# Reading the moving operand of the wide matrix products backwards, and writing their output backwards

## The chip, the cores and the metric

The kernel runs on one core of one Trainium2 chip. The metric is the device time of one execution in microseconds (us), as the median of several executions. The engines have short names in the profile: PE is TensorE (its matmuls), PEld its weight loads, DVE is VectorE, ACT is ScalarE, POOL is GpSimd, SP is SyncE, which here issues the DMAs.

## The reference: what is computed

Two layers of a streaming-encoder trunk over a sequence of 256 rows of 2048 features, all in float32. Each layer projects the input, runs three groups of heads (differential attention, banded chunk attention and an mLSTM), projects their outputs back, and adds a SwiGLU block, with a layer norm after each:

```
for li in range(DEPTH):                                   # DEPTH = 2
    proj = x @ w_in[li]
    ...
    mix = jnp.concatenate([ya, yb, yc], axis=-1) @ w_out[li]
    x = layer_norm(DEEPNORM_ALPHA * x + mix, ln1_g[li], ln1_b[li])
    ffn = (jax.nn.silu(x @ w_gate[li]) * (x @ w_up[li])) @ w_down[li]
    x = layer_norm(DEEPNORM_ALPHA * x + ffn, ln2_g[li], ln2_b[li])
```

## The kernel before

Five large weight matrices per layer (w_in, w_out, w_gate, w_up, w_down) are streamed once from memory. The output columns of each product are handled in groups of up to 1024 columns, and a group is two blocks: 512 and 512 columns nearly everywhere, 512 and 264 in the second group of w_in of each layer. The 256 rows of the sequence are two tiles t of 128. `run_groups` walks over the groups one after the other. Within a group a step k is one slice of 128 rows of the weights. For step k, `convert` brings the slice into a form of two parts: ScalarE writes the rounded upper part `whi` (line 225), VectorE the remainder `wlo` (line 226), both of type fp32r. The activations stand ready in the same two parts, transposed: `xth` and `xtl` (from x or from the mixed heads), or `gth` and `gtl` (from the SwiGLU gate).

The wide products are all issued by one line, 273. For each step and tile there are three part products (upper by upper, upper by remainder, remainder by upper), each on both blocks, so six instructions, which all add into the blocks' PSUM banks `mm`:

```
for i, (lt, wt) in enumerate(((xh, hi), (xh, lo), (xl, hi))):
    for b in bs:
        o, w = g["blocks"][b]
        nc.tensor.matmul(banks[t, b][:, 0:w], lt, wt[:, o:o + w],
```

The 128x128 activation block `lt` is the stationary operand, loaded by a weight load of its own ahead of each product. The weight block `wt`, 128 partitions by up to 512 columns, is the moving operand: its columns stream past the stationary one, and each column of it makes one column of output. When the last step of a bank is done, ScalarE or VectorE empties it. In most of a group the two blocks alternate, so that consecutive products go to different banks; in the last steps of a group (`so` of them) the order is by block, and consecutive products add into one bank.

Between the wide products the kernel's task list (`Tasks`) puts the small ones on TensorE: transposes (lines 296, 415, 649, 742) and the products of the heads (lines 520, 543, 550 to 552, 626, 672 to 674, 716, 750), which are plain float32 and go to banks named `aux`. Line 633 adds, on VectorE, a bias that is stored reversed: it reads `brev` with a step of -1; line 725 does the same operation in the other attention with a bias read forwards. Line 172 issues nine products on zeros at the very start.

What sets the order is the list of groups and steps written out in `run_groups`; every engine works through its own instruction queue in that order and waits only on data.

Of the kernel before, what the change touches and what calls it, by code (L numbers as in the profile page):

```python
# [135 lines left out]
class Trunk:  # L136
# [96 lines left out]
    def run_groups(self, groups):  # L233

        nc = self.nc
        self.steps, self.pairs, self.raws, self.whl = [], [], {}, {}
        for g in groups:
            g["base"] = len(self.steps)
            for k in range(g["nk"]):
                self.steps.append((g, k))  # L240
                if k % 2 == 0:
                    self.pairs.append(g["src"](k))
        for p in range(RAW_BUFS):
            self.load_pair(p)
            for c in {1: (1,), 2: (2, 3)}.get(p, ()):
                for t in range(NT):
                    self.load_x(nc.sync, t, c)
        done = 0
        for g in groups:
            nk, nb, si, so = g["nk"], len(g["blocks"]), g.get("skew_in", 1), g.get("skew_out", 1)  # L250
            allb = tuple(range(nb))
            order = [(k, t, allb) for t in range(NT) for k in range(si)]
            order += [(k, t, allb) for k in range(si, nk - so) for t in range(NT)]
            order += [(k, t, (b,)) for t in range(NT) for b in allb for k in range(nk - so, nk)]
            banks = {}
            g["start"]()
            for (k, t, bs) in order:
                j = g["base"] + k
                if (k, t, bs[-1]) == (nk - 1, NT - 1, nb - 1) and "mid" in g:
                    g["mid"]()  # L260
                xh, xl = g["lhs"](k, t)
                ahead = AHEAD if k >= nk - so or k < si else FAR_AHEAD
                while done < min(j + ahead + 1, len(self.steps)):
                    self.convert(done)
                    done += 1
                hi, lo = self.whl[j]
                for b in bs:
                    if (t, b) not in banks:
                        banks[t, b] = self.psum.tile([P, 512], F32, name="mm", tag="mm", bufs=MM_BUFS)
                for i, (lt, wt) in enumerate(((xh, hi), (xh, lo), (xl, hi))):  # L270
                    for b in bs:
                        o, w = g["blocks"][b]
                        nc.tensor.matmul(banks[t, b][:, 0:w], lt, wt[:, o:o + w],  # L273
                                         start=(k == 0 and i == 0), stop=(k == nk - 1 and i == 2))
                g["progress"] = k + 1
                if k == nk - 1:
                    for b in bs:
                        g["evac"](t, b, banks[t, b])
                if "after" in g and bs[-1] == nb - 1:
                    g["after"](k, t)  # L280
                if bs[-1] == nb - 1:
                    self.tasks.tick(g.get("budget", BUDGET) * g["width"] / 1024)
# [843 lines left out]
```

## Time and profile before

| | |
|---|---|
| time, median of 3 executions | 2342.06 us (2341.08 to 2342.38) |
| profiled execution, its own time | 2341.18 us |
| its span, first to last instruction | 2339.4 us |
| TensorE, share of the span with a product in flight | 99% |
| VectorE, ScalarE, GpSimd | 64%, 44%, 2% |
| mean granted TensorE clock | 0.998 of full speed |
| wide products (line 273) | 9792 instructions: 9600 of 512 columns, 192 of 264 |

The profiled execution lies 0.9 us below the median, within the spread of the three. A matmul's busy time counts from its start to the modelled end of its last output, and consecutive matmuls overlap; what a product costs in a stream of products is therefore the distance from one start to the next, not its duration.

### The profile page before, as it was taken

What the parts mean: (1) busy time and instruction counts of PE and PEld (TensorE: products, weight loads), DVE (VectorE), ACT (ScalarE), POOL (GpSimd) and SP (SyncE); (2) the same over time, 40 slices, a digit from 0 to 9 for tenths busy, and PEclk for the clock granted to TensorE, in tenths of its full rate; (3) what the DMA queues carried; (4) which work ended last, traced back from release to release, by engine and by line L of the source; (5) the groups of instructions that cost most, each with busy time, mean ns of one, the idle gap of its engine ahead of it and who ended that gap; (6) DMA issues with size and microseconds to landing.
All of it is one profiled execution on the core that took longest, in us unless ns stands there. A gap on an engine that the chain in (4) does not pass through costs nothing.

```text
span 2339.4 us, 27628 instructions
## 1 busy us (share of the span) xinstructions
PE 2318.4 (99%) x10538; PEld 1905.5 (81%) x10538; DVE 1498.3 (64%) x2360; ACT 1034.5 (44%) x1303; POOL 55.1 (2%) x120
## 2 busy tenths in 40 slices
PE   9999999999999999999999999999999999999997
PEld 7887788888888888888888877888888888888886
DVE  5755455777766447766577454557677664577765
ACT  5645554444444334444345454544444433444432
POOL 0001200000000000000000021000000000000000
PEclk9999999999999999999999999999999999999999
DMA  8654345565555555555556544555655555556553
GB/s 280 202 187 168 133 164 201 185 224 181 194 201 197 196 188 192 186 207 189 177 182 212 182 144 152 172 198 200 209 185 198 198 192 190 193 180 212 184 196 109
DMA packets 178933, 441.15 MB, mean 189 GB/s; under 512 B 15120, under 2 KB 22256, under 8 KB 177776
## 3 DMA queue, kind: packets, MB, share of 16 engines
q1 hardware_dynamic: 178656, 439.32, 55.5%
q8 instruction: 82, 1.34, 0.2%
q14 instruction: 51, 0.42, 0.1%
q10 hardware_dynamic: 144, 0.07, 0.0%
HBM read 437.25 MB, written 2.10 MB: 188 GB/s over the span
## 4 chain that ended last, share of the span: by engine, by line
PE 96%; DVE 2%; POOL 1%; ACT 1%; DMA 0%; issue 0%; SPq 0%; POOLq 0%
PE mm L273 92%; PE aux L296 1%; PE aux L543 1%; PE aux L415 1%; POOL mixc L610 1%; DVE x L341 0%; PE aux L716 0%; PE aux L626 0%; DVE bst L320 0%; DMA raw<-w_in 0%; ACT whi L225 0%; POOL rs L332 0%; POOL ve L330 0%; DVE wlo L226 0%; PE aux L750 0%
## 5 line engine op out<-in xcount | busy, mean ns | idle before, releaser
L226 DVE TENSOR_TENSOR wlo<-raw,whi 128x1024 fp32r<-128x1024 f32 (+2 forms) x817 | 985.8, 1212 | 705.0 <-ACT whi L225 700.9
L225 ACT CAST whi<-raw 128x1024 fp32r<-128x1024 f32 (+2 forms) x817 | 852.6, 1045 | 1172.5 <-PE mm L273 1142.9
L273 PE MATMUL mm<-whi,xth 128*128 128x512 f32 (+1 forms) x2560 | 812.6, 392 | 0.5 <-ACT whi L225 0.3
L273 PE MATMUL mm<-wlo,xth 128*128 128x512 f32 (+1 forms) x2560 | 799.1, 387 | 0.0
L273 PE MATMUL mm<-whi,xtl 128*128 128x512 f32 (+1 forms) x2560 | 798.2, 387 | 0.0
L273 PEld LDWEIGHTS mm<-whi,xtl 128*128 128x128 f32 x2560 | 476.2, 188 | 100.0 <-DVE xtl L287 0.6
L273 PEld LDWEIGHTS mm<-wlo,xth 128*128 128x128 f32 x2560 | 476.5, 188 | 98.8
L273 PEld LDWEIGHTS mm<-whi,xth 128*128 128x128 f32 x2560 | 467.0, 188 | 96.3 <-issue 4.0
L273 PE MATMUL mm<-whi,gtl 128*128 128x512 f32 x704 | 222.0, 389 | 0.0
L273 PE MATMUL mm<-whi,gth 128*128 128x512 f32 x704 | 222.0, 389 | 0.0
L273 PE MATMUL mm<-wlo,gth 128*128 128x512 f32 x704 | 221.9, 389 | 0.0
L407 DVE STREAM_TRANSPOSE gtr<-sil 32x128 f32<-32x128 f32 x704 | 213.0, 303 | 11.2
L273 PEld LDWEIGHTS mm<-whi,gth 128*128 128x128 f32 x704 | 132.1, 188 | 27.7
L273 PEld LDWEIGHTS mm<-whi,gtl 128*128 128x128 f32 x704 | 132.1, 188 | 27.5
L273 PEld LDWEIGHTS mm<-wlo,gth 128*128 128x128 f32 x704 | 132.1, 188 | 27.3
L330 POOL TENSOR_SCALAR ve<-mv 128x1 f32<-128x1 f32 x8 | 4.7, 590 | 1756.6 <-DVE mv L328 1756.5
L286 ACT CAST xth<-aux 128x512 fp32r<-128x512 f32 (+1 forms) x58 | 28.8, 511 | 29.0 <-PE aux L296 25.6
L287 DVE TENSOR_TENSOR xtl<-aux,xth 128x512 fp32r<-128x512 f32 (+1 forms) x58 | 33.5, 592 | 4.3 <-ACT xth L286 4.0
L1088 DVE TENSOR_TENSOR gtl<-gtr,gth 128x512 fp32r<-128x512 f32 x44 | 29.9, 681 | 0.7
L1035 ACT ACTIVATE sil<-mm 128x512 f32<-128x512 f32 x44 | 25.9, 594 | 9.9 <-PE mm L273 9.9
L1038 DVE TENSOR_TENSOR sil<-mm,sil 128x512 f32<-128x512 f32 x44 | 28.2, 682 | 1.4 <-ACT sil L1035 1.4
L341 DVE SCALAR_TENSOR_TENSOR x<-x,rs,lnb 128x512 f32<-128x512 f32 (+1 forms) x40 | 24.7, 639 | 2.8 <-POOL rs L332 2.7
(154 smaller groups left out, 677.1 us busy)
## 6 DMA issues: line engine op xcount, KB each, us to landing
raw<-w_gate SPq DMA_DIRECT2D x176, 512.0 KB, 3.7
raw<-w_up SPq DMA_DIRECT2D x176, 512.0 KB, 4.6
raw<-w_down SPq DMA_DIRECT2D x88, 1024.0 KB, 5.1
raw<-w_in SPq DMA_DIRECT2D x78, 1024.0 KB, 4.9
raw<-w_out SPq DMA_DIRECT2D x32, 1024.0 KB, 5.2
raw<-w_in SPq DMA_DIRECT2D x52, 512.0 KB, 4.1
raw<-w_in SPq DMA_DIRECT2D x16, 256.0 KB, 3.9
lng<-ln_g SPq DMA_DIRECT2D x4, 1024.0 KB, 7.8
```

What stands on the lines that cost most here:

```text
L225: nc.scalar.copy(out=hi[:, s], in_=src[:, s])
L226: nc.vector.tensor_tensor(out=lo[:, s], in0=src[:, s], in1=hi[:, s].bitcast(F32), op=ALU.subtract)
L273: nc.tensor.matmul(banks[t, b][:, 0:w], lt, wt[:, o:o + w], start=(k == 0 and i == 0), stop=(k == nk - 1 and i == 2))
L286: self.nc.scalar.copy(out=hi, in_=ps)
L287: self.nc.vector.tensor_tensor(out=lo, in0=ps, in1=hi.bitcast(F32), op=ALU.subtract)
L296: self.nc.tensor.transpose(out=ps[:, i * P:(i + 1) * P], in_=s, identity=self.ident)
L341: nc.vector.scalar_tensor_tensor(out=z, in0=z, scalar=rs, in1=lb[:, s], op0=ALU.mult, op1=ALU.add)
L407: self.nc.vector.transpose(out=out[32 * j:32 * j + 32, 0:n, 32 * i:32 * i + 32], in_=in_[32 * i:32 * i + 32, 0:n, 32 * j:32 * j + 32])
L415: self.nc.tensor.transpose(out=ps[:, i * P:(i + 1) * P], in_=stg[:, i * P:(i + 1) * P], identity=self.ident)
L1035: nc.scalar.activation(out=box["s", t], in_=bank, func=AF.Silu)
L1038: nc.vector.tensor_tensor(out=g, in0=bank, in1=g, op=ALU.mult)
L1088: nc.vector.tensor_tensor(out=lo, in0=gt, in1=hi.bitcast(F32), op=ALU.subtract)
```

## The change

The moving operand of each wide product is read with a step of -1, from its last column to its first. The output columns are addressed with a step of -1 too, so each product column lands where it landed before. Stationary operands, numbers of columns, accumulation flags, banks, and all other instructions stay as they are. The list of instructions of each engine (TensorE, VectorE, ScalarE, GpSimd, SyncE) is the same before and after, row by row; only the access patterns inside line 273's matmuls differ.

```
@@ -270,7 +270,7 @@
                 for i, (lt, wt) in enumerate(((xh, hi), (xh, lo), (xl, hi))):
                     for b in bs:
                         o, w = g["blocks"][b]
-                        nc.tensor.matmul(banks[t, b][:, 0:w], lt, wt[:, o:o + w],
+                        nc.tensor.matmul(banks[t, b][:, 0:w][:, ::-1], lt, wt[:, o:o + w][:, ::-1],
                                          start=(k == 0 and i == 0), stop=(k == nk - 1 and i == 2))
```

## Rows read from the trace of the kernel before

**Rows 1.** The page: busy time of each engine, share of the span, instructions.

```profile
PE 2318.4 (99%) x10538; PEld 1905.5 (81%) x10538; DVE 1498.3 (64%) x2360; ACT 1034.5 (44%) x1303; POOL 55.1 (2%) x120
```

**Rows 2.** The chain that ended last on the page, by engine and by line.

```profile
PE 96%; DVE 2%; POOL 1%; ACT 1%; DMA 0%; issue 0%; SPq 0%; POOLq 0%
PE mm L273 92%; PE aux L296 1%; PE aux L543 1%; PE aux L415 1%; POOL mixc L610 1%; DVE x L341 0%; PE aux L716 0%; PE aux L626 0%; DVE bst L320 0%; DMA raw<-w_in 0%; ACT whi L225 0%; POOL rs L332 0%; POOL ve L330 0%; DVE wlo L226 0%; PE aux L750 0%
```

**Rows 3.** The same chain in order of time, longest pieces: start us, us, what.

```profile
479.13 683.00 PE mm L273 x3012
...
1639.61 678.90 PE mm L273 x2994
```

**Rows 4.** Waits by engine: waiting engine and line, releaser, us, times, longest.

```profile
PE aux L296 <- DVE x L341: 2.2, 6, 0.7
PE aux L543 <- DVE mixa L758: 1.6, 2, 0.8
...
PE mm L273 <- ACT whi L225: 0.3, 1, 0.3
...
ACT whi L225 <- PE mm L273: 1142.9, 705, 5.7
```

**Rows 5.** Groups of TensorE by form: shapes, xcount | busy us, mean ns.

```profile
L273 PE MATMUL mm<-whi,xth 128*128 128x512 f32 x2496 | 804.3, 395 | 0.5 <-ACT whi L225 0.3
...
L273 PE MATMUL mm<-whi,gth 128*128 128x512 f32 x704 | 222.0, 389 | 0.0
...
L273 PE MATMUL mm<-whi,xth 128*128 128x264 f32 x64 | 18.1, 282 | 0.0
...
L172 PE MATMUL aux<-warm 128*128 128x512 bf16 x9 | 4.0, 631 | 1.2 <-DVE mhalf L174 1.2
```

**Rows 6.** Timeline of TensorE, products of 512 columns: start us, us, instruction, count.

```profile
2279.79 0.62 PE L273 MATMUL mm<-whi,gtl 128*128 128x512 f32 x2
2280.24 0.62 PE L273 MATMUL mm<-whi,gth 128*128 128x512 f32 x2
...
2309.71 0.62 PE L273 MATMUL mm<-whi,gtl 128*128 128x512 f32 x2
2310.16 0.39 PE L273 MATMUL mm<-whi,gth 128*128 128x512 f32 x1
2310.39 0.39 PE L273 MATMUL mm<-wlo,gth 128*128 128x512 f32 x1
```

**Rows 7.** Timeline of TensorE, pairs of one product of 512 and one of 264 columns.

```profile
65.71 0.51 PE L273 MATMUL mm<-whi,xtl 128*128 128x512 f32 x2
66.06 0.51 PE L273 MATMUL mm<-whi,xth 128*128 128x512 f32 x2
...
71.66 0.51 PE L273 MATMUL mm<-wlo,xth 128*128 128x512 f32 x2
```

**Rows 8.** Stretches, line 273 alone: us, PE busy (x), PEld busy (x), PEclk, DMA share, GB/s.

```profile
479.00:1162.00 683.00, 683.00 (x3013) 565.21 (x3014) 1.00 0.57 194
```

**Rows 9.** Timeline of TensorE, plain float32 products of 193 columns, two per row.

```profile
255.95 0.49 PE L550 MATMUL aux<-cv,work 128*128 128x193 f32 x2
256.27 0.49 PE L551 MATMUL aux<-cv,work 128*128 128x193 f32 x2
...
257.58 0.49 PE L552 MATMUL aux<-cv,work 128*128 128x193 f32 x2
```

**Rows 10.** Timeline of TensorE, the nine products of 512 columns on zeros.

```profile
1.17 4.02 PE L172 MATMUL aux<-warm 128*128 128x512 bf16 x9 [1.17 <-DVE mhalf L174]
```

**Rows 11.** Groups of VectorE by form: bias read forwards (line 725) and backwards (line 633).

```profile
L725 DVE CUSTOM_DVE_ANT_0 work<-aux,cst_sb 128x256 f32<-128x256 f32 x16 | 6.1, 418 | 0.0
...
L633 DVE CUSTOM_DVE_ANT_0 work<-aux,brev 128x256 f32<-128x256 f32 x12 | 4.6, 420 | 3.0 <-PE aux L626 3.0
...
L725 DVE CUSTOM_DVE_ANT_0 work<-aux,cst_sb 128x128 f32<-128x128 f32 x16 | 4.3, 287 | 4.9 <-PE aux L716 4.7
...
L633 DVE CUSTOM_DVE_ANT_0 work<-aux,brev 128x128 f32<-128x128 f32 x12 | 3.1, 287 | 6.3 <-PE aux L626 6.3
```

More of the change, by code (lines that the diff above doesn't have):

```diff
@@ L272, in run_groups @@
                         o, w = g["blocks"][b]
-                        nc.tensor.matmul(banks[t, b][:, 0:w], lt, wt[:, o:o + w],
+                        nc.tensor.matmul(banks[t, b][:, 0:w][:, ::-1], lt, wt[:, o:o + w][:, ::-1],
                                          start=(k == 0 and i == 0), stop=(k == nk - 1 and i == 2))
```

## The prediction

> **What bounds the kernel now.** I read the page's busy shares first: TensorE has a product in flight for 99% of the span, VectorE 64%, ScalarE 44% [rows 1]. A busy matmul row is not proof of a bound, so the chain that ended last comes next: 96% of it is TensorE, and 92% is line 273 alone [rows 2]. In order of time the chain has two unbroken pieces of wide products, 683 us and 679 us long [rows 3]. The list of waits agrees: the wide products wait 0.3 us for their converted weights in the whole run, while ScalarE's conversions wait 1142.9 us for the products to free a buffer [rows 4]. So the time is the number of wide products times the distance from one to the next, plus some 140 us of other things, and whatever the change does to that distance goes into the time at full size.
>
> The distance comes from the timeline. From 2279.79 to 2309.71 us there are 66 steps of two products of 512 columns: 29.92 / 132 = 226.7 ns each [rows 6]. In the group with blocks of 512 and 264 columns, 17 pairs take 71.66 - 65.71 = 5.95 us, so 350 ns a pair, and 350.0 - 226.7 = 123.3 ns for the product of 264 columns [rows 7]. The difference of 248 columns is 103.4 ns: **0.417 ns a column**, and 226.7 - 512 x 0.417 = **13.2 ns fixed** a product. [...] There are 2496 x 3 + 704 x 3 = 9600 of 512 columns and 64 x 3 = 192 of 264 [rows 5], where of three part products of the same count one stands: 9600 x 0.2267 + 192 x 0.1233 = 2176 + 24 = 2200 us of the span of 2339.4. The duration of 389 ns [rows 5] is not the cost: consecutive products overlap.
>
> **The change, part by part.** It removes and adds no instruction. Three things could change in a product.
>
> *Reading the moving operand backwards.* [...] The nearest row is on another engine. Line 633 adds a bias that it reads with step -1, line 725 does the same operation with a forward bias: 420 against 418 ns for 256 columns, and 287 against 287 ns for 128 [rows 11]. A backward read of this memory costs nothing there. This row is only a weak bound, because VectorE takes (420 - 287) / 128 = 1.04 ns a column, 2.5 times TensorE's 0.417: whatever fetches two columns together would not show on it. Lower bound 0.
>
> *Writing PSUM backwards.* No row of before shows any engine writing PSUM backwards. The bounds are 0, and the rate of the slowest products here. The plain float32 products of 193 columns start 1.63 us apart over ten, so 163 ns each or 0.845 ns a column [rows 9]; the nine products at the start overlap too, and (4.02 - 0.631) / 8 = 0.424 us between starts is 0.827 ns a column [rows 5, 10]. So this machine has products at one column per 0.42 ns and at one per 0.83 to 0.85 ns. I price the upper bound of both operands with the second.
>
> *Accumulation.* A column of a bank is added to again by a later product. When consecutive products add into one bank, column c of the next follows column c of the last by one product, 226.7 ns, in either direction, since both run backwards. Last column and release of the bank come at the same moment of the product too, so the evacuations, the conversions that wait for the products, and the DMAs behind them see nothing.
>
> I take 0 for all three. The order of columns changes neither how many values are fetched nor which of them are neighbours in time; with even block widths (512, 264) and blocks that start at column 0 or 512, a stream cut into pairs or fours from its far end has the same pairs and fours as from its near end, each only turned round. Sum: 2339.4 us of span unchanged, with 1.8 us around it as in the profiled run (2341.18), and the median of before was 0.9 us above that: **2342 us**. What hides the change, if it takes longer, is nothing: there is no slack on TensorE, so each extra ns a product is 9.8 us of time. A measurement of this kernel can tell about 0.2%, 4.7 us, from no change, which is 0.48 ns a product, one column's time. That is the point from which any surcharge decides.
>
> [...]
>
> **The rivals.**
>
> 1. *Half rate (slower).* [...] Time: 512 x 0.845 = 432.6 ns, 205.9 more, x 9600 = 1977 us; 264 x 0.845 = 223, 99.8 more, x 192 = 19 us; together **4338 us**. With 0.827 ns a column it is 196.7 and 95 more, so 4249 us; with twice 0.417 plus the fixed 13.2 it is 213.5 and 110 more, so 4413 us. All other engines would be idle more; none would become the bound.
>
> 2. *A fixed surcharge (slower).* The turn at the start of each product (a start address at the far end, or a break in the stream) costs something once. The nearest size is the 13.2 ns that a product already has beside its columns: 0 to 9792 x 13.2 ns = 129 us, so up to 2471 us, in the middle 2407 us. Against it: each product already starts at an address of its own, in another bank or another weight block than the last, and no row shows a product's cost hanging on where it starts.
>
> [...]
>
> 4. *Faster.* Only the fixed 13.2 ns could shrink, if the last-written end of one product and the first of the next came to suit each other; half of it gone would be 65 us, 2277 us. Nothing speaks for it.
>
> 5. *The change doesn't do what it says.* Reversing both sides is the same arithmetic as reversing none, and a program builder could fold it away. The time would be 2342 us, as in my forecast.
>
> **How the numbers follow.** No change, with case 5 in it: 0.64. Half rate: 0.20, as nothing in the rows excludes it and a written rule can be read that way. Fixed surcharge above 0.48 ns: 0.07. Breaks at lines: 0.04. More than half rate lost: 0.03. Faster: 0.02. So faster by over 0.2% 0.02, within 0.64, slower 0.34. The likeliest case's own range is 2337 to 2347 us (2342 with 0.2% on each side). With the fixed surcharge and the line breaks it holds only 0.75, so the range has to reach to the half rate and its upper price: 2337 to 4415 us. This is wide because the answer has two places, not because times between them are likely.
>
> **What would show it.** Right: in the profile after, the two-product steps of the timeline stay at 0.45 us and the pairs of 512 and 264 columns at 0.35 us, mean durations stay at 389 and 282 ns, and the chain's long pieces at 683 and 679 us. Wrong by rival 1: steps of 0.83 to 0.88 us, while the small products on the same engine keep theirs, and ScalarE's wait for the products about 2000 us longer. [...] The prediction falls if the distance between starts of wide products moves by more than half a ns.

## The result and the profile after

The kernel with the change takes 2399.70 us (median of 4, 2399.58 to 2400.24), the kernel before 2341.72 us in the same series: ratio 1.0248, 95% interval 1.0230 to 1.0266. It is slower by 58 us. The forecast was no change.

The page of the kernel after, busy time of each engine, answers to [rows 1]; below it the two longest pieces of the chain that ended last (start us, us, what), which answer to [rows 3]:

```profile
PE 2379.4 (99%) x10538; PEld 1910.4 (80%) x10538; DVE 1500.7 (63%) x2360; ACT 1029.7 (43%) x1303; POOL 54.7 (2%) x120
```

```profile
488.32 702.88 PE mm L273 x3012
...
1678.20 698.67 PE mm L273 x2994
```

TensorE's busy time grew by 61 us, that of the other engines changed by at most 5 us. The long pieces hold as many products as before and take 702.88 / 3012 = 233.4 ns each instead of 683.00 / 3012 = 226.8: **6.6 ns a product**. The two pieces together are 39.7 us longer, of 58.4 us in the span (2397.8 against 2339.4). The rest of the span, with the other 3594 products of 512 columns, is 18.7 us longer, 5.2 ns for each; why it is less there wasn't followed.

The timeline of TensorE after, first for blocks of 512 and 264 columns, from 2299.69 us on for two of 512 (start us, us, instruction, count), answers to [rows 6, 7]:

```profile
66.26 0.52 PE L273 MATMUL mm<-whi,xth 128*128 128x512 f32 x2
...
71.61 0.52 PE L273 MATMUL mm<-whi,xth 128*128 128x512 f32 x2
...
2299.69 0.63 PE L273 MATMUL mm<-whi,gth 128*128 128x512 f32 x2
...
2309.49 0.63 PE L273 MATMUL mm<-whi,gth 128*128 128x512 f32 x2
```

Twenty-one steps of two products take 9.80 us, 466.7 ns a step, so 233.3 ns a product. Fifteen steps of a 512 and a 264 take 71.61 - 66.26 = 5.35 us, 356.7 ns a step where 350 ns stood: 6.7 ns a pair, what the product of 512 columns alone accounts for; by this the product of 264 columns pays nothing, and run 3 measures it by itself. That already fits neither a fixed price for each product (13 ns a pair) nor a price for each column (10 ns a pair).

The list of waits after answers to [rows 4]: ScalarE's conversions wait 74 us longer for the products, and the products wait no longer for the conversions (0.4 us). The granted clock of the long stretch is 1.00 as in [rows 8].

```profile
ACT whi L225 <- PE mm L273: 1216.7, 719, 6.0
...
PE mm L273 <- ACT whi L225: 0.4, 1, 0.4
```

### The profile page after: what moved, and what is told of

The parts are those of the page before. It is cut to its first block, busy times and chain, and to the rows that moved or that the text cites. A ratio compares the mean times of both kernels' runs of the same rounds, so it can differ in the third digit from the quotient of the medians.

```text
span 2397.8 us, 27622 instructions
## 1 busy us (share of the span) xinstructions
PE 2379.4 (99%) x10538; PEld 1910.4 (80%) x10538; DVE 1500.7 (63%) x2360; ACT 1029.7 (43%) x1303; POOL 54.7 (2%) x120
## 4 chain that ended last, share of the span: by engine, by line
PE 96%; DVE 2%; POOL 1%; ACT 1%; DMA 0%; issue 0%; SPq 0%; POOLq 0%
PE mm L273 92%; PE aux L296 1%; PE aux L543 1%; PE aux L415 1%; DVE x L341 0%; POOL mixc L610 0%; PE aux L716 0%; PE aux L626 0%; DVE bst L320 0%; DMA raw<-w_in 0%; ACT whi L225 0%; PE aux L750 0%; POOL rs L332 0%; POOL ve L330 0%; DVE wlo L226 0%
## 5 line engine op out<-in xcount | busy, mean ns | idle before, releaser
L273 PE MATMUL mm<-whi,xth 128*128 128x512 f32 (+1 forms) x2560 | 830.1, 400 | 0.4 <-ACT whi L225 0.4
L273 PE MATMUL mm<-whi,xtl 128*128 128x512 f32 (+1 forms) x2560 | 816.6, 395 | 0.0
L273 PE MATMUL mm<-wlo,xth 128*128 128x512 f32 (+1 forms) x2560 | 816.5, 395 | 0.0
L273 PE MATMUL mm<-whi,gth 128*128 128x512 f32 x704 | 227.4, 397 | 0.0
L273 PE MATMUL mm<-whi,gtl 128*128 128x512 f32 x704 | 227.3, 397 | 0.0
L273 PE MATMUL mm<-wlo,gth 128*128 128x512 f32 x704 | 227.2, 397 | 0.0
```

Source lines behind the costliest of these rows:

```text
L273: nc.tensor.matmul(banks[t, b][:, 0:w][:, ::-1], lt, wt[:, o:o + w][:, ::-1], start=(k == 0 and i == 0), stop=(k == nk - 1 and i == 2))
```

## The experiments

### 1 and 2: reading backwards alone, writing backwards alone

The converted weights are stored mirrored, column c of a step at width - 1 - c. Then one of the two sides can run backwards by itself with the reference's output. Of the edits, the ScalarE line stands here; VectorE's line, left out, changes in the same way.

```
             d = slice(w - s.stop, w - s.start)
-            nc.scalar.copy(out=hi[:, s], in_=src[:, s])
+            nc.scalar.copy(out=hi[:, d][:, ::-1], in_=src[:, s])
...
+                        m = g["width"] - o - w
# run 1
+                        nc.tensor.matmul(banks[t, b][:, 0:w], lt, wt[:, m:m + w][:, ::-1],
# run 2
+                        nc.tensor.matmul(banks[t, b][:, 0:w][:, ::-1], lt, wt[:, m:m + w],
```

> The converted weights are stored mirrored, so that line 273 reads them backwards and writes PSUM forwards; the output is that of the reference. Theory R (the surcharge of about 6 ns a wide product comes from reading the moving operand backwards): about 2399 us, 1.025 of before, pairs of 512-column products 0.467 us apart. Theory W (it comes from writing PSUM backwards): about 2342 us, pairs 0.453 us apart. Theory B (each side pays a part, or both together are needed): between, or both this run and the next near 2342 us.

> The converted weights are stored mirrored as in the run before, line 273 reads them forwards and writes PSUM backwards. Theory W: about 2399 us, pairs 0.467 us apart. Theory R: about 2342 us, pairs 0.453 us apart. Theory B: between, or near 2342 us in both. If both runs are near 2399 us the mirrored storing itself, or a cost that either side triggers once, is behind it.

Measured: reading backwards alone 2398.92 us, ratio 1.0244 (1.0227 to 1.0262). Writing backwards alone 2341.63 us, ratio 0.9999 (0.9990 to 1.0009). The chain's long pieces, of run 1 and then of run 2:

```profile
488.35 702.87 PE mm L275 x3012
...
1677.59 698.67 PE mm L275 x2994
```

```profile
479.36 682.98 PE mm L275 x3012
...
1639.33 678.91 PE mm L275 x2994
```

Theory R holds, W and B fall: **the whole cost is on the side of the read**. In this kernel writing PSUM backwards is free, and so is storing the weights mirrored by ScalarE and VectorE, which run 2 does as well.

### 3: bare streams, with nothing beside them

A kernel of its own issues streams of 120 products each to two alternating banks, from one converted tile, with four stationary blocks in turn. It computes nothing of the reference.

```
for i in range(120):
    nc.tensor.matmul(wr(ps[i % 2][:, 0:n]), st[:, (i // 2 % 4) * P:(i // 2 % 4 + 1) * P],
                     rd(mv[:, i % 2 * 1024:i % 2 * 1024 + n]), ...)
```

> Not the reference's computation: streams of 120 matmuls each with nothing beside them, to measure the distance between starts for one choice of direction, width, type and access pattern at a time. Theory S (a fixed cost at the start of a product): backward minus forward is about 6.6 ns at 512 columns and at every smaller width down to 128. Theory C (a cost per column or per line of columns): 6.6 ns at 512, 3.4 ns at 264, 1.7 ns at 128. Theory N (contention with the engines that convert weights beside it): nothing at any width, since no other engine runs here.

In the timeline of TensorE below, one row is one stream; its distance between starts is the next row's start less its own, divided by 120. `ff` reads and writes forwards, `bb` both backwards, `rb` reads backwards, `wb` writes backwards; an `h` ahead is bf16. `lin_r` reads pieces of 4 (first), 16 (second) and 64 columns (third) from the last piece to the first, forwards within each; `in_r` reads the pieces in forward order, backwards within each.

```profile
37.77 27.36 PE L40 MATMUL ff_o<-mv,st 128*128 128x512 f32 x120
64.97 28.17 PE L40 MATMUL bb_o<-mv,st 128*128 128x512 f32 x120
92.97 28.16 PE L40 MATMUL rb_o<-mv,st 128*128 128x512 f32 x120
120.97 27.38 PE L40 MATMUL wb_o<-mv,st 128*128 128x512 f32 x120
148.19 26.56 PE L40 MATMUL ff_o<-mv,st 128*128 128x496 f32 x120
...
438.32 14.56 PE L40 MATMUL ff_o<-mv,st 128*128 128x264 f32 x120
452.72 14.56 PE L40 MATMUL bb_o<-mv,st 128*128 128x264 f32 x120
467.12 14.56 PE L40 MATMUL rb_o<-mv,st 128*128 128x264 f32 x120
...
662.12 26.07 PE L40 MATMUL hff_o<-mvb,stb 128*128 128x512 bf16 x117
688.03 26.06 PE L40 MATMUL hbb_o<-mvb,stb 128*128 128x512 bf16 x118
713.93 26.06 PE L40 MATMUL hrb_o<-mvb,stb 128*128 128x512 bf16 x117
...
902.43 28.17 PE L40 MATMUL lin_r_o<-mv,st 128*128 128x512 f32 x120
930.43 27.38 PE L40 MATMUL in_r_o<-mv,st 128*128 128x512 f32 x120
957.65 27.36 PE L40 MATMUL lin_w_o<-mv,st 128*128 128x512 f32 x120
...
1012.05 28.16 PE L40 MATMUL lin_r_o<-mv,st 128*128 128x512 f32 x120
1040.05 32.16 PE L40 MATMUL in_r_o<-mv,st 128*128 128x512 f32 x120
1072.04 27.40 PE L40 MATMUL lin_w_o<-mv,st 128*128 128x512 f32 x120
...
1126.48 27.36 PE L40 MATMUL lin_r_o<-mv,st 128*128 128x512 f32 x120
1153.68 28.17 PE L40 MATMUL in_r_o<-mv,st 128*128 128x512 f32 x120
```

The table has some streams more, whose rows are left out above.

| stream | ns from start to start |
|---|---|
| fp32r, 512 columns: ff, bb, rb, wb | 226.7, 233.3, 233.3, 226.8 |
| fp32r, 496 columns: ff, bb, wb | 220.0, 226.7, 223.3 |
| fp32r, 448 columns: ff, bb, wb | 202.7, 206.6, 202.7 |
| fp32r, 384 columns: ff, bb, wb | 173.6, 177.8, 173.4 |
| fp32r, 264 columns: ff, bb, wb | 120.0, 120.0, 121.3 |
| fp32r, 256 columns: ff, bb, wb | 119.9, 118.4, 119.9 |
| bf16, 512 columns: ff, bb | 215.9, 215.8 |
| pieces of 4: reversed order, reversed within | 233.3, 226.8 |
| pieces of 16: reversed order, reversed within | 233.3, 266.6 |
| pieces of 64: reversed order | 226.7 |

The surcharge of the kernel is there with no other engine at work, so theory N (contention) falls. Theory S falls at 264 columns, and theory C, which asked for 3.4 ns there, too: the surcharge is neither fixed nor in proportion. It is 6.7 ns at 512 and at 496 columns, about 4 at 448 and 384, nothing at 264, and at 256 reading backwards is even 1.5 ns faster. Counted at the 0.4167 ns a column that lie between 512 and 496 columns forwards ((27.20 - 26.40) us / 120 / 16), the forward time beside the columns isn't the same for every width either: 13.3 ns at 512, 16.0 at 448, 10.0 at 264 (the kernel's pairs of 512 and 264 gave 13.3 there, 123.3 - 110.0). Writing backwards, free at 512 columns, took 3.3 ns more at 496 and 1.3 at 264. bf16 products of 512 columns have no surcharge. How long a column of bf16 takes wasn't measured; by the author's estimate, with fp32r's 213.3 ns for 512 columns, 2.6 ns are left beside them (215.9 - 213.3), where fp32r has 13.3 (a few of the 120 records of the bf16 streams are missing from the trace, but the streams start at even distances). What the order of the pieces shows is odder still: reading eight pieces of 64 columns backwards is free (226.7 ns), reading backwards within each four columns is free (226.8), and what hurts most is neither (266.6, backwards within pieces of 16).

### 4: the number of stationary columns, and where the operands start

Bare streams again, 512 columns, 120 products; the number of stationary columns m, the start column of the stationary and of the moving operand, and the pieces vary.

```
nc.tensor.matmul(ps[i % 2][0:m, 0:512], st[:, q:q + m], rd(mv[:, o:o + 512]), ...)   # q from so, o from ro
```

> Not the reference's computation: streams of 120 fp32r matmuls of 512 columns with nothing beside them; the number of stationary columns, the start columns of both operands and the order of the pieces vary. Theory L (the time a product takes beside its columns, 13.3 ns forwards and 20 ns backwards, comes from the weight load that reads the same memory beside it, and the direction changes how often the two reads meet): both shrink in step with the stationary columns, to about a quarter (3 and 5 ns) at 32 columns, and they depend on where the operands start. Theory J (the moving read alone loses time where its address steps back): 13.3 and 20 ns at every number of stationary columns and for every start that is a multiple of 16 columns.

The timeline of TensorE, one row a stream: m of 128, 96, 64, 32 forwards, 128 and 32 backwards, then, forwards, stationary starts of 1, 4 and 8 columns:

```profile
37.49 27.36 PE L42 MATMUL colsaf_o<-mv,st 128*128 128x512 f32 x120
64.69 27.77 PE L42 MATMUL colsbf_o<-mv,st 128*96 128x512 f32 x120
92.30 27.76 PE L42 MATMUL colscf_o<-mv,st 128*64 128x512 f32 x120
119.89 27.96 PE L42 MATMUL colsdf_o<-mv,st 128*32 128x512 f32 x120
147.69 28.16 PE L42 MATMUL colsab_o<-mv,st 128*128 128x512 f32 x120
...
231.69 28.16 PE L42 MATMUL colsdb_o<-mv,st 128*32 128x512 f32 x120
259.69 28.05 PE L42 MATMUL soffaf_o<-mv,st 128*128 128x512 f32 x120
...
315.27 28.16 PE L42 MATMUL soffcf_o<-mv,st 128*128 128x512 f32 x120
343.26 28.16 PE L42 MATMUL soffdf_o<-mv,st 128*128 128x512 f32 x120
```

Forwards it is 226.7 ns at 128 stationary columns, 230 at 96 and 64, and 231.7 at 32 ((147.69 - 119.89) / 120); backwards 233.3 at 128 and 32. The weight load itself is busy for 188 ns at 128 columns and 109 at 32. So theory L's main claim is wrong: the time beside the columns doesn't shrink with the weight load, it even grows. Its second claim is right: a *forward* product whose stationary operand starts 4 columns off took 233.3 ns (343.26 - 315.27, over 120), as much as a backward one; 8 and 16 columns off gave the same, and 64 columns off cost next to nothing (227.2 ns, row not shown). Theory J, by which forward products are 226.7 ns for every such start, falls.

### 5 and 6: do the orders of the bare streams hold in the kernel?

```
+                        ov, mv = banks[t, b][:, 0:w], wt[:, o:o + w]
+                        if w == 512:      # run 5: c=64, [:, ::-1, :]; run 6: c=16, [:, :, ::-1]
+                            ov, mv = (v.rearrange("p (a c) -> p a c", c=64)[:, ::-1, :] for v in (ov, mv))
+                        nc.tensor.matmul(ov, lt, mv,
```

> The products of 512 columns read and write their eight pieces of 64 columns from the last to the first, forwards within a piece; the output is that of the reference. In the bare stream this order of reading cost nothing (226.7 ns between starts). If what the bare stream shows holds in the kernel: 2342 us, ratio 1.000. If any backward step costs, or what counts is the far end where a product starts: 2342 to 2400 us.

> The products of 512 columns read and write their 32 pieces of 16 columns in forward order, but backwards within a piece; the output is that of the reference. In the bare stream this order was the costliest one, 266.6 ns between starts. If that holds in the kernel: 40 ns x 9600 = 384 us more, about 2726 us. If the cost is one for a backward direction as such, whatever the pieces: about 2400 us.

Run 5: 2341.26 us, ratio 0.9999 (0.9989 to 1.0008). Reading backwards by pieces of 64 columns is free in the kernel too, although each product starts near the far end of its block; the start at the far end is not the cause. Run 6, a single execution: 2711.31 us, 369 us more where 384 was expected. Its timeline:

```profile
2599.88 0.70 PE L276 MATMUL mm<-whi,gth 128*128 128x512 f32 x2
...
2605.22 0.70 PE L276 MATMUL mm<-wlo,gth 128*128 128x512 f32 x2
```

Ten steps in 5.34 us, 267 ns a product, as in the bare stream (266.6).

### 7 and 8: the starts of the two operands against each other

Run 7 is the kernel before, all forwards, with one line more; run 8 is bare streams of 64 products over a grid of starts.

```
         self.wp = pool("wp")
+        self.wp.tile([P, 8], F32, name="wpad")
```

> The kernel before, all reads and writes forwards, with one unused tile of 8 columns ahead of the weight buffers, so that converted weights and the gate's activations gth and gtl start 32 bytes later and xth, xtl do not. The output is that of the reference. Theory P (the part of a product beside its columns depends on how the starts of moving and stationary operand lie to each other): the 7488 products of 512 columns with xth or xtl take 233.3 ns instead of 226.7, those with gth or gtl, where both have moved alike, stay at 226.7: 7488 x 6.7 ns = 50 us more, about 2392 us. Theory A (the start of the moving operand alone counts): all 9600 are slower, about 2406 us. Theory D (only the direction counts): 2342 us.

> Not the reference's computation: streams of 64 fp32r matmuls of 512 columns with nothing beside them, where the starts of the stationary and of the moving operand take each of 0, 4, 8, 16, 32, 48, 64 and 96 columns, forwards, and the moving start alone backwards. Theory P: where both are shifted alike, 226.7 ns as without a shift; where one is shifted against the other by 4 to 48 columns, 229 to 234 ns; a shift by 64 counts as none. Theory A: the stationary start changes nothing. Backwards 233 ns or more for every start by either.

Run 7: 2383.56 us, ratio 1.0180 (1.0163 to 1.0197), without a single backward access. Its timeline of TensorE, first products with xth and xtl, then with gth and gtl:

```profile
600.38 0.63 PE L274 MATMUL mm<-wlo,xth 128*128 128x512 f32 x2
...
603.18 0.63 PE L274 MATMUL mm<-wlo,xth 128*128 128x512 f32 x2
...
2300.12 0.62 PE L274 MATMUL mm<-whi,gth 128*128 128x512 f32 x2
...
2303.74 0.61 PE L274 MATMUL mm<-whi,gtl 128*128 128x512 f32 x2
```

Six steps of two products with xth and xtl take 2.80 us, 233.3 ns a product. Eight steps with gth and gtl, where both operands moved alike, take 3.62 us, 226.3 ns, as before within the rounding of the two starts. The loss of 42.5 us is less than the 50 expected, 5.7 ns a product in the mean over 7488. The two long pieces of the chain account for 26.0 us of it (696.00 and 691.88 us against 683.00 and 678.90), which is the full 6.6 ns for each of their 3948 products with xth or xtl; the other 3540 lose 4.7 ns in the mean. Among those, 93 pairs of 512 and 264 columns in a row take 33.07 us against 32.89, so only 1.9 ns a pair: the loss isn't the same in every mix of widths. Why was not followed. Theory P holds for streams of 512 columns in the kernel, with its own control; A and D fall.

The timeline of run 8. Names are f (forwards) or b (backwards), then a letter for the stationary start and one for the moving start: a to h are 0, 4, 8, 16, 32, 48, 64, 96 columns. The distance is the next row's start less the row's own, over 64.

```profile
25.87 14.67 PE L42 MATMUL faa_o<-mv,st 128*128 128x512 f32 x64
40.38 14.99 PE L42 MATMUL fab_o<-mv,st 128*128 128x512 f32 x64
55.20 15.10 PE L42 MATMUL fac_o<-mv,st 128*128 128x512 f32 x64
70.14 14.81 PE L42 MATMUL fad_o<-mv,st 128*128 128x512 f32 x64
...
114.58 14.71 PE L42 MATMUL fag_o<-mv,st 128*128 128x512 f32 x64
129.13 15.09 PE L42 MATMUL fah_o<-mv,st 128*128 128x512 f32 x64
144.06 15.09 PE L42 MATMUL fba_o<-mv,st 128*128 128x512 f32 x64
158.99 14.95 PE L42 MATMUL fbb_o<-mv,st 128*128 128x512 f32 x64
...
291.82 14.71 PE L42 MATMUL fcc_o<-mv,st 128*128 128x512 f32 x64
306.37 15.10 PE L42 MATMUL fcd_o<-mv,st 128*128 128x512 f32 x64
...
972.99 15.09 PE L42 MATMUL bca_o<-mv,st 128*128 128x512 f32 x64
987.92 15.10 PE L42 MATMUL bcb_o<-mv,st 128*128 128x512 f32 x64
```

With the stationary operand at 0, moving starts of 0, 4, 8 columns give 226.7, 231.6, 233.4 ns, and 64 columns 227.3, as good as none. With the moving operand at 0 and the stationary one at 4 columns it is 233.3 (fba). Both shifted by 8 give 227.3 (fcc). For starts that are multiples of 16 columns the whole grid goes by the moving start less the stationary one, counted modulo 64 four-byte columns (a difference of 64 counts as 0): 226.7 to 227.3 ns at a difference of 0, 229 at 16, 232 to 233 at 32, 233 at 48. With starts of 4 and 8 this has exceptions: 4 and 4 take 230.9 ns, while 4 and 8 (either way), and a stationary start of 4 with a moving one of 32, take 226.7 to 227.2. Backwards, all eight streams, with a stationary start of 8, are at 233.3 to 233.4. No stream of the grid is below 226.7.

### 9: backwards and a bad start together

The changed kernel with the one line of run 7.

> The changed kernel, backwards reads and writes, with the same unused tile of 8 columns as in the run before, so that xth and xtl lie 32 bytes off the weights they stream against; the output is that of the reference. Theory P1 (a backwards read has lost the favourable relation of the two reads once and for all, so a bad start costs it nothing more): about 2400 us, products with xth at 233.3 ns as with gth. Theory P2 (direction and start are two costs that add): about 2400 + 42 = 2442 us, products with xth at about 240 ns.

Measured: 2398.61 us, ratio 1.0244 (1.0227 to 1.0261). The chain's long piece is the one of the kernel after, 702.87 us for 3012 products:

```profile
488.66 702.87 PE mm L274 x3012
```

Theory P1 holds: for a start 8 columns off, the two costs don't add. That they are two ways to lose the same thing is argued from this. In run 4 some starts did add a little to a backward read: moving starts of 1, 2 and 32 columns took 235.5, 236.7 and 236.7 ns.

## Why the prediction was wrong

**The bound was read rightly.** The time is the number of wide products times the distance between starts, and a change of the distance shows nearly in full: 6.6 ns on 9600 products would be 63 us, and the span grew by 58. The threshold of 0.48 ns a product was right as well; the change cost more than ten times that.

**The step that failed** is "I take 0 for all three", in its first term, the backward read: 6.6 ns a product of 512 columns. Two arguments stood under it. One was the row of VectorE, which reads backwards for nothing [rows 11]; the text itself called it a weak bound. The other was that a stream cut into pairs or fours has the same pairs turned round. Run 3 shows that this is true and not enough: turning round each four columns is free, but reversing the order of the fours costs the whole 6.7 ns. And under rival 2 the prediction said that no row shows a product's cost hanging on where it starts; runs 4, 7 and 8 show that it does.

**What stands in its place.** The 13.2 ns beside a product's columns were taken as a constant of the machine; at 512 columns they are the best case of something that depends on both operands. Shown for bare streams of 512 columns: with forward reads the time beside the columns is 13.3 to 14 ns when moving and stationary operand start alike modulo 64 columns (17.6 with both at 4), and mostly 15 to 23 ns when they don't (runs 4, 8). With a backward read it is 20 ns at nearly every start tried (runs 4 and 8; 22 to 23 ns at a few in run 4), and at none of them clearly less. That the kernel before sat in the best case is inferred, as no run lists the addresses: its products were 226.7 ns apart, and moving the weights by 8 columns cost the products with xth, not those with gth (run 7). The backward read took it out of that case. Reading by pieces of 64 columns backwards fits the same relation, and is free (226.7 ns in run 3, 2341.26 us in run 5); by pieces of 32 it took 232.5 ns (run 4, row not shown), about what a difference of 32 columns costs (232 to 233 ns, run 8).

What the time is lost to, no run shows; theory L's picture, in which the moving read meets the weight load's read, was the author's guess. For it stands that the place of the stationary operand alone changes a product's time: 226.7 ns with both operands at 0, 233.3 with only the stationary one moved to 4 columns (run 8). Against a plain count of meetings stands that fewer stationary columns don't make it less: 226.7 ns at 128 of them, 231.7 at 32 (run 4). A product of this type without a weight load wasn't tried. Open too are how the surcharge goes with the width, 264 columns paying nothing, and why pieces of 16 read backwards within cost 40 ns (266.6 against 226.7, run 3).

**The rivals.** The half rate is out: backwards, 16 columns more cost 6.67 ns (496 and 512, run 3), still 0.417 ns a column. The written rule that its chance of 0.20 leans on is shown by no run; in the runs a backward write cost nothing (run 2) and a backward read 6.6 ns (run 1). One of the two rows that were taken for half-rate products was misread, too: the nine products at the start are bf16, and run 3 has bf16 products of the same 512 columns 215.9 ns apart, not 424. The granted clock reads 1.00 from 2 to 4 us, while the nine run, so their slowness stays open. Breaks at lines, with a chance of 0.04: that a read breaks at lines of columns, and what a break costs, is shown by no run; run 3 showed 6.7 ns a product for the reversed order of fours and none for turning each four round. A change that is folded away is out with the 58 us. That only the 13.2 ns could shrink, as the faster rival has it, was the author's estimate; no fp32r stream of 512 columns came below 226.7 ns (runs 3, 4, 8). The write side costs nothing in this kernel: run 2 took 2341.63 us against 2342.21. The fixed surcharge named the right size, 0 to 13.2 ns a product and 2407 us in its middle, with a chance of 0.07, but not the right law: the pairs with 264 columns grew by one surcharge, not two, and bf16 has none. The time of 2399.7 us lies inside the range only because the range was drawn out to the half rate.

## What to carry to other kernels

A stream of fp32r products of 512 columns was at its best here, 226.7 to 227.3 ns a product, when moving and stationary operands started at the same place modulo 64 four-byte columns and the moving one was read forwards (both at 4 columns took 230.9); a tile of 8 columns in the wrong pool cost this kernel 1.8% (run 7), so look at the starts whenever a pool's layout changes. If an order must be reversed, reverse it in the PSUM write, in the storing of the weights, or by pieces of 64 columns: all three measured as free in this kernel (2341.63 us with the first two in run 2, 2341.26 with the third in run 5). At other widths measure first, as 496 columns written backwards paid 3.3 ns (run 3). And a "fixed" cost read from one kernel's rows is only the cost at that kernel's layout; ask what it could depend on before holding it constant.

## What the runs showed of the hardware that wasn't expected

- Two ways to write PSUM out of order, backwards and by reversed pieces of 16 columns (226.8 and 227.0 ns against 226.7), cost a product of 512 columns next to nothing.
- A bf16 product of 512 columns takes 215.9 ns, an fp32r one 226.7 at best: 5% between the types.
- Reading pieces of 16 columns in order but backwards within each is far dearer (266.6 ns) than reading everything backwards (233.3).
